# Attention projections taken two groups at a time, 512 columns to a bank, weights in four pieces out of the common slots

## The chip, the core and the metric

The kernel runs on one core of a Trainium2 chip. The metric is the device time of one execution in microseconds (us), median of three runs. The profile is one further execution of the same program, recorded by the hardware profiler. PE is the matrix engine (TensorE), PEld its loading of stationary operands, DVE the vector engine, ACT the scalar engine, POOL GpSimd, SP the queue that issues most DMAs.

## What is computed

One layer of a streaming encoder over 1024 positions of width 1024, in float32. The normalized input is projected to many column groups at once, three token mixers work on them, gates merge their outputs, and a SwiGLU block follows:

```python
h = rms_norm(x, g_mix[l])
z = h @ w_in[l]
aq, ak, av, bq, bk, bv, iq, ik, iw, cx, cy, gt = split_cols(z)
y_a = chunk_relpos_attention(rms_norm(aq), rms_norm(ak), av, rel_bias)      # 4 heads, band of 9 chunks
q_b = apply_rope(rms_norm(bq)); k_b = apply_rope(rms_norm(bk))
score = sum_h w_i[h] * relu(q_i[h] . k_i)                                   # indexer, 4 heads
y_b = attention of q_b over the top 256 keys of score
y_c = rglru_branch(cx, cy, ...)
merged = sum_b sigmoid(gt_b) * (y_b @ w_branch_b)
x = x + merged @ w_out[l]
x = x + (silu(g_) * u_) @ w_ffn_out[l]
```

The change is in the projections of aq, ak, av, bq, bk, bv: six groups of 256 columns.

## The kernel before

Every product is made of three matmuls: both operands are split into a high part (by ACT, L101) and a rest (by DVE, L102), and `mm3` adds high x high, high x rest and rest x high (L117 to L119). A weight piece is loaded by `load_split` (L104): a DMA on the SP queue into a tile "r", then the high part "h" on ACT and the rest "l" on DVE. So a piece of weights named wz appears as wzr (raw), wzh and wzl, each 4 KB to a partition (128x1024).

**Slots.** All such tiles lie in 50 slots. `ring` is a set of 7 for weights alone, `sl` one of 43 for all else: score and relu tiles, softmax tiles P and transposed ones PT, sorted keys, bias and mask tiles, z tiles. A `get` takes the slot that was freed longest ago, a `free` puts it at the end of the list:

```python
i = self.free_list.pop(0)
...
self.free_list.append(i)
```

A tile in a slot waits for the last reader of the tile that had it. `z_group` (L318) takes its two pieces (128x4x256, half of the 1024 input rows each) from `ring`.

**Projection.** `z_batch` (L329) computes four of the eight blocks of 128 positions: two blocks share a PSUM bank of 512 columns as two halves of 256. A block is 24 matmuls of 256 columns (8 input slices by 3). ACT copies a whole bank out (L335). `head_rstd` (L339) then makes the head norms: a square on ACT, a sum on DVE, a power on POOL, a multiplication on DVE. `qk_A` makes queries and keys of two heads of branch A, `v_group` the values, `qk_B` queries and keys of branch B with their rotation. Each is called once for each of the six groups: 6 x 8 x 24 = 1152 matmuls of 256 columns.

**What lies around it.** From about 48 us PE makes the indexer's scores: 24 S tiles of `dots` (L242, L243), two banks in turn; ACT applies relu (L310), DVE weights and adds (L312, L314). The relu tile of one S tile lies in a slot of `sl` until DVE has read it. After that, DVE finds the 256th largest score of each row in 32 rounds of a bitwise search ("K" steps; counts at L643, on ACT at L655), while attention A runs: A0 and A1 are its two pairs of heads, with 8 blocks of 2 heads each. In `attention` (L396) each S tile is read by DVE (L406, adds bias or mask, takes the minimum), ACT takes exp (L409), DVE scales (L412), PE transposes to T banks (L418), ACT copies to PT (L419), PE multiplies with v (L426). Gates ("G" steps, wg weights, 512 columns), branch C, then attention B (B0, B1) follow, then merge and SwiGLU, which is PE work alone with its loads beside it.

**The order.** The string ORDER says which step's program text comes next: K a round of the search, A a block of attention A, G a gate, Z a projection, C, B, T, W, F the rest. The scheduler of the tile framework then orders each engine's instructions within the window that the string gives.

## Time and profile before

| | us |
|---|---|
| median of 3 runs (1515.85 to 1518.37) | 1517.07 |
| the profiled execution itself | 1517.05 |
| its span, from the first to the last instruction | 1515.3 |
| PE busy | 1469.1 |
| DVE busy | 1119.1 |
| ACT busy | 762.9 |

The time of a run is the span and 1.75 us around it. Busy times overlap between engines; those of PE are longer than the spacing of its matmuls, since the next one starts while the last is still draining, so the spacing of starts says what a matmul costs in a stream.

### The profile page before, as it was taken

The page shows a single profiled execution, that of the slowest core. Times are in us where ns is not written, and L with a number is a line of the kernel's source. Part 1 is how long each engine was busy: PE and PEld are TensorE (multiplying, and loading weights), DVE is VectorE, ACT ScalarE, POOL GpSimd, SP SyncE. Part 2 cuts the span into 40 slices and gives each one's busy share as a digit, 9 for nine tenths or more (in the row PEclk, how much of TensorE's full clock was granted, in tenths as well). Part 3 has the DMA queues.
Part 4 walks back from the last instruction along what each step waited for, and adds up shares of the span by engine and source line. Part 5 has one row for each costly group of instructions (what it writes and reads, how often), then busy time and mean ns, then how long its engine had stood idle before and what let it go on. Part 6 is the DMA issues. An engine that isn't in the chain of part 4 may idle for free.

```text
span 1515.3 us, 19935 instructions
## 1 busy us (share of the span) xinstructions
PE 1469.1 (97%) x7556; PEld 1228.5 (81%) x7556; DVE 1119.1 (74%) x1985; ACT 762.9 (50%) x1208; POOL 109.5 (7%) x161
## 2 busy tenths in 40 slices
PE   6999899999999998999999989999999999999999
PEld 5898688989788876788888868888888888888887
DVE  7989999869666779767889776555555556578972
ACT  6557768775778656443214663333333333344340
POOL 1220011210000200110000200000000000000000
PEclk9999999999999999999999999999999999999999
DMA  7011212122111121357552412323232323697532
GB/s 289 29 46 54 87 32 102 39 70 85 56 53 45 42 102 53 125 181 298 216 189 75 153 59 96 111 97 112 98 111 98 111 97 126 230 386 263 190 125 89
DMA packets 52240, 182.59 MB, mean 120 GB/s; under 512 B 6000, under 2 KB 6128, under 8 KB 52144
## 3 DMA queue, kind: packets, MB, share of 16 engines
q1 hardware_dynamic: 38448, 135.17, 25.9%
q0 software_dynamic: 11968, 43.00, 7.2%
q10 hardware_dynamic: 1728, 3.15, 0.5%
q8 instruction: 59, 0.97, 0.3%
q14 instruction: 37, 0.30, 0.1%
HBM read 135.94 MB, written 45.35 MB: 120 GB/s over the span
## 4 chain that ended last, share of the span: by engine, by line
PE 75%; DVE 14%; ACT 5%; issue 3%; DMA 2%; POOL 0%; POOLq 0%; ACTq 0%; SPq 0%; DVEq 0%
PE B L119 15%; PE B L118 15%; PE B L117 15%; PE G L118 7%; PE G L119 7%; PE G L117 6%; DVE key L643 3%; PE T L426 2%; PE T L118 1%; PE T L117 1%; PE T L119 1%; PE T L418 1%; PE S L117 1%; PE S L118 1%; PE S L119 1%
## 5 line engine op out<-in xcount | busy, mean ns | idle before, releaser
L118 PE MATMUL B<-hl,fwh 128*128 128x512 f32 x528 | 205.8, 392 | 1.5 <-DVE hl L1026 1.5
L117 PE MATMUL B<-hh,fwh 128*128 128x512 f32 x528 | 203.4, 393 | 1.6 <-ACT hh L1025 1.3
L119 PE MATMUL B<-hh,fwl 128*128 128x512 f32 x528 | 198.8, 391 | 1.9 <-DVE fwl L102 1.9
L117 PEld LDWEIGHTS B<-hh,fwh 128*128 128x128 f32 x528 | 99.8, 189 | 23.5 <-ACT hh L1025 2.2
L119 PEld LDWEIGHTS B<-hh,fwl 128*128 128x128 f32 x528 | 99.8, 189 | 23.1 <-DVE fwl L102 2.3
L118 PEld LDWEIGHTS B<-hl,fwh 128*128 128x128 f32 x528 | 99.8, 189 | 22.9 <-DVE hl L1026 2.2
L118 PE MATMUL G<-wzl,hTh 128*128 128x256 f32 x384 | 111.3, 290 | 5.3 <-DVE wzl L102 5.3
L117 PE MATMUL G<-wzh,hTh 128*128 128x256 f32 x384 | 110.8, 291 | 1.3 <-ACT wzh L101 0.6
L119 PE MATMUL G<-wzh,hTl 128*128 128x256 f32 x384 | 110.8, 289 | 0.0
L102 DVE TENSOR_TENSOR fwl<-s,fwh 128x1024 fp32r<-128x1024 f32 x44 | 53.7, 1223 | 74.1 <-PE B L118 74.1
L118 PE MATMUL B<-fol,foh 128*128 128x512 f32 x264 | 102.9, 390 | 0.0
L119 PE MATMUL B<-foh,fol 128*128 128x512 f32 x264 | 101.9, 389 | 0.0
L117 PE MATMUL B<-foh,foh 128*128 128x512 f32 x264 | 101.1, 389 | 0.0
L655 ACT ACTIVATE junk_s<-score,ngS 128x1024 int8<-128x1024 f32 (+2 forms) x78 | 77.5, 994 | 17.5 <-DVE ngS L653 13.5
L118 PEld LDWEIGHTS G<-wzl,hTh 128*128 128x128 f32 x384 | 74.6, 194 | 7.1 <-DVE wzl L102 6.1
L119 PE MATMUL G<-hTh,wgl 128*128 128x512 f32 x192 | 75.8, 395 | 2.0 <-DVE wgl L102 2.0
L117 PEld LDWEIGHTS G<-wzh,hTh 128*128 128x128 f32 x384 | 74.6, 195 | 3.2 <-ACT wzh L101 1.1
L117 PE MATMUL G<-hTh,wgh 128*128 128x512 f32 x192 | 75.8, 395 | 0.0
L118 PE MATMUL G<-hTl,wgh 128*128 128x512 f32 x192 | 75.4, 393 | 0.0
L119 PEld LDWEIGHTS G<-wzh,hTl 128*128 128x128 f32 x384 | 74.8, 195 | 0.3 <-issue 0.2
L101 ACT ACTIVATE fw<-fb 128x512 fp32r<-128x512 f32 x22 | 13.9, 632 | 117.0 <-PE B L119 117.0
L101 ACT ACTIVATE foh<-fa 128x1024 fp32r<-128x1024 f32 x33 | 35.0, 1061 | 57.5 <-DMA fa<-pd 37.7
(486 smaller groups left out, 3847.7 us busy)
## 6 DMA issues: line engine op xcount, KB each, us to landing
fw<-in_w_fo SPq DMA_DIRECT2D x33, 512.0 KB, 5.7
fa<-pd SPq DMA_DIRECT2D x33, 512.0 KB, 5.5
gl<-gd SPq DMA_DIRECT2D x24, 512.0 KB, 5.9
fa<-in_w_fi SPq DMA_DIRECT2D x22, 512.0 KB, 3.5
fb<-in_w_fi SPq DMA_DIRECT2D x22, 512.0 KB, 3.6
pd<-act POOLq DMA_DIRECT2D x22, 512.0 KB, 5.3
ga<-in_w_g SPq DMA_DIRECT2D x18, 512.0 KB, 3.6
x<-in_x SPq DMA_DIRECT2D x16, 512.0 KB, 5.9
```

The lines of the kernel that those rows point to most:

```text
L101: S.activation(hi, raw, AF.Copy)
L102: (eng or V).tensor_tensor(lo, raw, hi.bitcast(F32), op=OP.subtract)
L117: PE.matmul(o, lhsT=lh, rhs=rh, start=first, stop=False, **kw)
L118: PE.matmul(o, lhsT=lh, rhs=rl, start=False, stop=False, **kw)
L119: PE.matmul(o, lhsT=ll, rhs=rh, start=False, stop=last, **kw)
L418: PE.transpose(pt[:, b - c0], P[:, 128 * b:128 * b + 128], ident)
L426: PE.matmul(o[64 * e:64 * e + 64, :], lhsT=v[(b0 + b) // 4][:, (b0 + b) % 4, h, :], rhs=PT[e][:, b, :], start=b == 0, stop=b == nb - 1, sk ...
L643: V.tensor_scalar(o[:, 0:(i + 1) * 128], (keys or score)[i], ap[:, j:j + 1], 0.0, op0=op, op1=OP.add, accum_out=self.cnt[:, j:j + 1])
L655: S.activation(junk_s[:, 0:(i + 1) * 128], score[i], AF.Sign, bias=self.ng.bitcast(F32)[:, j:j + 1], accum_out=self.cnt[:, j:j + 1])
```

## The change

`z_group`, `z_batch`, `qk_A`, `v_group`, `qk_B` go. `z_pair` takes two groups together: (q and k of A0, v of A), (q and k of A1, q and k of B0), (v of B, q and k of B1). Its weights come as four pieces (128x2x512, a quarter of the input rows each), the same 12 loads of 512 KB in all, but out of `zw`, which is `sl`: the common slots, with no slots of their own. A block is 24 matmuls of 512 columns into a whole bank, 576 in all. ACT copies each bank out in two copies of 256 columns, 48 in all where there were 24 of 512. The head norms of the first pair come behind the whole pair, and `rope_B` is called where a Z step of B stood. In ORDER some G steps stand later among the K and A steps before the first Z, and one more behind the third Z. The weights' layout on the host follows.

```diff
-ORDER = ("KAAGKKKAKKAKAKKKKKKAGGGAKKKKAYAKGGAGAKKKKKKKAKKKAZ"
-         "AAAKKGKGZKKKKBCBGBCBCBCBBBZBBFBFBGGBBBBTTWFFWWFFWWW")
+ORDER = ("KAAGKKKAKKAKAKKKKKKAGGGAKKKKAYAKAGAKKKKGKKKAKKKGAZ"
+         "AAAKKKGZKKKKBCBGBCBCBCBBBZGBBFBFBGGBBBBTTWFFWWFFWWW")
...
-    def z_group(gi):
-        ws = [load_split(w_zg[gi, kk], (128, 4, 256), "wz") for kk in range(2)]
-        return ws
...
+    def z_pair(gi, names):
+        ws = [load_split(w_zg[gi, q], (128, 2, 512), "wz", zw) for q in range(4)]
+        zs = []
+        for g in range(2):
+            z = [sl.get((128, 4, 4, 64), F32, n) for n in names]
+            for j in range(4):
+                t = 4 * g + j
+                p = gbank()
+                for k in range(KD):
+                    hh, hl = hT[k]
+                    wh, wl = ws[k // 2]
+                    mm3(p, hh[:, 128 * t:128 * t + 128], hl[:, 128 * t:128 * t + 128], wh[:, k % 2], wl[:, k % 2],
+                        k == 0, k == KD - 1)
+                for n in range(2):
+                    S.activation(z[n][:, j].rearrange("p h d -> p (h d)"), p[:, 256 * n:256 * n + 256], AF.Copy)
+            zs.append(z)
+        for wh, wl in ws:
+            zw.free(wh, wl)
+        return [[z[n] for z in zs] for n in range(2)]
...
-    zA = [qk_A(0)]
-    vA = v_group(2)
-    def steps_zA():
-        zA.append(qk_A(1))
+    zw = sl
+    qk0, vA = z_pair(0, ("zA", "v"))
+    zA, zB, vB = [qk0], [], []
+    for z in qk0:
+        head_rstd(z)
+
+    def steps_zA():
+        qk1, b0 = z_pair(1, ("zA", "zB"))
+        for z in qk1:
             head_rstd(z)
...
-        zB.append(qk_B(3, tabs))
+        rope_B(zB[0], tabs)
         yield
-        vB.extend(v_group(5))
+        v, b1 = z_pair(2, ("v", "zB"))
+        vB.extend(v)
         yield
-        zB.append(qk_B(4, tabs))
+        rope_B(b1, tabs)
+        zB.append(b1)
         sl.free(*tabs)
         yield
```

Three places of the engines' orders follow. In these rows a name ends in the number of the buffer or of the instruction that wrote it, and "waits" names what the row waits for.

The first place is PE at the beginning of the indexer's scores. Before, S tiles (S_642, S_648) stand among matmuls of the first projection (G_889), whose weights wzh_11 to wzl_15 came from `ring`:

```order
L119 MATMUL G_889<-wzh_14_834,hTl_14_97 128x256
L117 MATMUL G_889<-wzh_14_834,hTh_15_98 128x256
L242 MATMUL S_642<-kih_39_315,qi_35_311 128x384 [waits Activation_49]
L242 MATMUL S_648<-kih_39_315,qi_36_312 128x384
L118 MATMUL G_889<-wzl_15_835,hTh_15_98 128x256
L119 MATMUL G_889<-wzh_14_834,hTl_16_99 128x256
L117 MATMUL G_889<-wzh_11_828,hTh_1_84 128x256
L118 MATMUL G_889<-wzl_12_829,hTh_1_84 128x256
```

In the changed order the projection's first matmul (G_852, out of wzh_79) comes when 17 of the 24 S tiles (up to S_758) have been issued, and the next ones stand two tiles later, behind wzl_80:

```order
L242 MATMUL S_758<-kih_39_315,qi_35_311 128x512 [waits Activation_49]
L243 MATMUL S_758<-kil_40_316,qi_35_311 128x512
L242 MATMUL S_758<-kih_39_315,qi_35_311 128x384
L243 MATMUL S_758<-kil_40_316,qi_35_311 128x384
L117 MATMUL G_852<-wzh_79_828,hTh_1_84 128x512 [waits Activation_49]
L117 MATMUL G_879<-wzh_79_828,hTh_1_84 128x512
L242 MATMUL S_766<-kih_39_315,qi_36_312 128x512 [waits Activation_49]
```

Here the projection no longer stands between the first 17 S tiles, and two banks of it start together as pieces arrive.

The second place is DVE, where the weight pieces are split (L102). Before, wzl_15 and wzl_18 stand among the rotation of the indexer's queries, ahead of the scores:

```order
L213 TENSOR_TENSOR qi_37_313<-T_461,qi_37_313 64x512 [waits Activation_49]
L102 TENSOR_TENSOR wzl_15_835<-wzr_13_832,wzh_14_834 128x1024 [waits DMAHW6_49,Activation_49]
L213 TENSOR_TENSOR qi_36_312<-T_452,qi_36_312 64x512 [waits Activation_49]
L282 TENSOR_TENSOR zq_45_477<-zq_45_477,t2_48_603 128x1024 [waits DVE_49]
L273 SCALAR_TENSOR_TENSOR zk_46_478<-zk_46_478,rsk_595,sm_68 128x64 [waits Pool_49]
```

Now the splits stand among the scores of the last three blocks of queries, the first with nine score rows to go:

```order
L314 SCALAR_TENSOR_TENSOR score_51_639<-relu_68_746,iw_310,score_51_639 128x768 [waits DVE_49,Activation_49]
L102 TENSOR_TENSOR wzl_80_829<-wzr_78_826,wzh_79_828 128x1024 [waits DMAHW7_49,Activation_49]
L314 SCALAR_TENSOR_TENSOR score_51_639<-relu_69_754,iw_310,score_51_639 128x768 [waits DVE_49,Activation_49]
L312 TENSOR_SCALAR score_52_640<-relu_70_763,iw_310 128x896 [waits Activation_49]
L102 TENSOR_TENSOR wzl_83_835<-wzr_81_832,wzh_82_834 128x1024 [waits DMAHW0_49,Activation_49]
```

The pieces have moved behind the rows that free their slots: wzr_78 is in the slot of relu_63, wzh_79 in that of relu_64, wzl_80 in that of relu_65, each of which DVE reads first.

The third place is PE at the second projection, at the end of A0. Before, its matmuls stand between S tiles (S_2242 is A0's last but one) with the weights of `ring`:

```order
L243 MATMUL S_2242<-kl_94_1413,qs_90_1409 128x256
L119 MATMUL G_2364<-wzh_39_2303,hTl_6_89 128x256
L117 MATMUL G_2364<-wzh_39_2303,hTh_7_90 128x256
L118 MATMUL G_2364<-wzl_40_2304,hTh_7_90 128x256
L119 MATMUL G_2364<-wzh_39_2303,hTl_8_91 128x256
L117 MATMUL G_2314<-wzh_42_2309,hTh_9_92 128x256 [waits Activation_49]
```

In the changed order all of A0's S tiles are ahead of it, and its third piece (wzl_148) stands behind T_2104, the product of A0's last block with v. These are the rows where the fourth piece (wzh_150, wzl_151) comes in:

```order
L118 MATMUL G_2170<-wzl_148_2132,hTh_11_94 128x512
L119 MATMUL G_2170<-wzh_147_2131,hTl_12_95 128x512
L117 MATMUL G_2143<-wzh_150_2137,hTh_13_96 128x512 [waits Activation_49]
L117 MATMUL G_2170<-wzh_150_2137,hTh_13_96 128x512
L118 MATMUL G_2143<-wzl_151_2138,hTh_13_96 128x512 [waits DVE_49]
L119 MATMUL G_2143<-wzh_150_2137,hTl_14_97 128x512
```

So the projection has moved behind A0. The slot of wzr_149 is that of PT_137 and the slot of wzh_150 that of PT_139, both read by T_2104; wzl_151 is in the slot of a bias tile of A0. From wzl_151 on, 154 of this projection's 192 matmuls are still to come, and then the transposes for A1.

## Rows read from the trace of the kernel before

**Rows 1.** The page of the profile: the span, and busy time of each engine.

```profile
span 1515.3 us, 19935 instructions
...
PE 1469.1 (97%) x7556; PEld 1228.5 (81%) x7556; DVE 1119.1 (74%) x1985; ACT 762.9 (50%) x1208; POOL 109.5 (7%) x161
```

**Rows 2.** Stretches: PE, PEld, DVE, ACT, POOL busy (instructions), PE clock, DMA share, GB/s.

```profile
0.00:48.00 48.00, 34.86 (x199) 31.90 (x200) 35.39 (x113) 28.87 (x83) 12.58 (x19) 1.00 0.59 228
48.00:75.00 27.00, 23.74 (x170) 21.47 (x170) 24.66 (x38) 16.80 (x32) 2.82 (x5) 1.00 0.13 40
75.00:119.00 44.00, 44.00 (x342) 42.73 (x341) 39.09 (x105) 23.57 (x32) 9.18 (x9) 1.00 0.15 49
119.00:199.00 80.00, 70.94 (x375) 56.98 (x375) 78.47 (x279) 57.59 (x118) 2.22 (x4) 0.96 0.17 61
188.00:195.60 7.60, 4.46 (x20) 3.79 (x20) 7.60 (x26) 5.09 (x12) 0.00 (x0) 0.72 0.00 1
600.00:1515.00 915.00, 902.74 (x3982) 742.75 (x3981) 626.05 (x798) 350.74 (x444) 45.04 (x85) 1.00 0.42 151
```

**Rows 3.** Timeline of PE, 256 columns: start, duration, engine, line, operation, tiles.

```profile
101.76 0.28 PE L119 MATMUL G<-wzh,hTl 128*128 128x256 f32 x1
...
103.92 0.28 PE L117 MATMUL G<-wzh,hTh 128*128 128x256 f32 x1
```

**Rows 4.** Timeline of PE, matmuls of 512 columns.

```profile
949.81 0.39 PE L118 MATMUL B<-hl,fw 128*128 128x512 f32 x1
...
961.82 0.39 PE L119 MATMUL B<-hh,fwl 128*128 128x512 f32 x1
```

**Rows 5.** Groups of DVE from 75 to 240 us: busy, mean ns, idle before.

```profile
L643 DVE TENSOR_SCALAR_CACHE_REDUCE key<-key,cdV 128x896 bf16<-128x896 bf16 x15 | 17.2, 1143 | 0.1
L643 DVE TENSOR_SCALAR_CACHE_REDUCE key<-key,cdV 128x640 bf16<-128x640 bf16 x15 | 13.1, 876 | 0.2
L643 DVE TENSOR_SCALAR_CACHE_REDUCE key<-key,cdV 128x512 bf16<-128x512 bf16 x15 | 11.2, 745 | 0.1
...
L643 DVE TENSOR_SCALAR_CACHE_REDUCE key<-key,cdV 128x384 bf16<-128x384 bf16 x15 | 9.1, 609 | 0.2
...
L406 DVE CUSTOM_DVE_ANT_0 P<-S,biasA 128x640 f32<-128x640 f32 x8 | 6.6, 820 | 1.2 <-PE T L418 0.7 <-PE T L426 0.6
```

**Rows 6.** Tile wzr: its DVE reader, and issue to landing of its DMA.

```profile
L102 DVE TENSOR_TENSOR wzl<-wzr,wzh x12: 1218/1224/1227, 47.9 to 480.6; 128x1024 fp32r<-128x1024 f32 x12
...
DMA to landing us min/median/max: 3.3/3.5/10.8
```

**Rows 7.** Groups of ACT from 0 to 600 us: two copies out of a bank.

```profile
L335 ACT ACTIVATE zA<-G 128x512 f32<-128x512 f32 x8 | 4.6, 598 | 1.1 <-PE G L119 1.1
...
L260 ACT ACTIVATE zq<-G 128x256 f32<-128x256 f32 x8 | 3.1, 382 | 10.9 <-PE G L119 10.9
```

**Rows 8.** Timeline of DVE, score rows of one block of 128 queries.

```profile
71.76 2.87 DVE L314 SCALAR_TENSOR_TENSOR score<-relu,iw,score 128x640 f32<-128x640 f32 x3
```

**Rows 9.** Timeline of DVE, second S tile of A0's seventh block.

```profile
193.33 0.82 DVE L406 CUSTOM_DVE_ANT_0 P<-S,biasA 128x640 f32<-128x640 f32 x1
```

**Rows 10.** Timeline of PE, first S tiles of A1 and of B0.

```profile
239.59 0.28 PE L242 MATMUL S<-kh,qs 128*128 128x256 f32 x1
...
369.85 0.28 PE L242 MATMUL S<-kh,qs 128*128 128x256 f32 x1
```

**Rows 11.** Timeline of PE, first and last S tile of B1.

```profile
535.68 0.28 PE L242 MATMUL S<-kh,qs 128*128 128x256 f32 x1
...
577.62 0.47 PE L242 MATMUL S<-kh,qs 128*128 128x512 f32 x1
```

**Rows 12.** Timeline of PE, a wait for a weight piece, and matmuls behind it.

```profile
193.40 0.39 PE L118 MATMUL G<-wzl,hTh 128*128 128x256 f32 x1 [3.13 <-DVE wzl L102]
...
194.13 0.41 PE L119 MATMUL G<-wzh,hTl 128*128 128x256 f32 x1
194.34 0.41 PE L117 MATMUL G<-wzh,hTh 128*128 128x256 f32 x1
```

More of the change, by code (lines that the diff above doesn't have):

```diff
@@ L317, in hybrid_kernel @@
     sl.free(*qi, kih, kil, ctab)
-    def z_group(gi):
-        ws = [load_split(w_zg[gi, kk], (128, 4, 256), "wz") for kk in range(2)]
-        return ws
-    def z_mm(ws, p, t):
-        for k in range(KD):
-            hh, hl = hT[k]
-            wh, wl = ws[k // 4]
-            mm3(p, hh[:, 128 * t:128 * t + 128], hl[:, 128 * t:128 * t + 128], wh[:, k % 4], wl[:, k % 4],
-                k == 0, k == KD - 1)
-    def z_batch(ws, g, name):
-        z = sl.get((128, 4, 4, 64), F32, name)
-        for a in range(2):
-            p = gbank((128, 2, 256))
-            for j in range(2):
-                z_mm(ws, p[:, j], 4 * g + 2 * a + j)
-            S.activation(z[:, 2 * a:2 * a + 2].rearrange("p t h d -> p (t h d)"), p.rearrange("p t c -> p (t c)"),
-                         AF.Copy)
-        return z
+    def z_pair(gi, names):
[17 more added lines that the diff above has]
+        return [[z[n] for z in zs] for n in range(2)]
     def head_rstd(z):
@@ L365, in to_stack @@
         return q, kh, kl
-    def done(ws):
-        for wh, wl in ws:
-            ring.free(wh, wl)
     ga8 = const.tile([128, 1], F32, name="ga8")
     V.tensor_scalar(ga8, smc("ga", 0), 0.125, None, op0=OP.mult)
-    def qk_A(gi):
-        ws = z_group(gi)
-        r = []
-        for g in range(2):
-            z = z_batch(ws, g, "zA")
-            head_rstd(z)
-            r.append(z)
-        done(ws)
-        return r
-    def v_group(gi):
-        ws = z_group(gi)
-        r = [z_batch(ws, g, "v") for g in range(2)]
-        done(ws)
-        return r
-    zA = [qk_A(0)]
-    vA = v_group(2)
-    def steps_zA():
-        zA.append(qk_A(1))
+    zw = sl
[6 more added lines that the diff above has]
+        for z in qk1:
+            head_rstd(z)
+        zA.append(qk1)
+        zB.append(b0)
         yield
@@ L564, in bm, with rope_B @@
         return ap[:, None, :].to_broadcast([128, n, ap.shape[-1]])
-    def qk_B(gi, tabs):
-        ws = z_group(gi)
-        r = []
-        for g in range(2):
-            z = z_batch(ws, g, "zB")
+    def rope_B(zs, tabs):
+        for g, z in enumerate(zs):
             head_rstd(z)
@@ L579, in qk_B @@
             V.tensor_add(z, z, t2)
-            r.append(z)
             sl.free(t2)
-        done(ws)
-        return r
     def steps_zB():
@@ L1475, in _layout @@
     pair = lambda q, k, p: np.concatenate([blk(q + 128 * p, 128), blk(k + 128 * p, 128)], 2)
-    zg = [pair(COL_AQ, COL_AK, 0), pair(COL_AQ, COL_AK, 1), blk(COL_AV, 256),
-          pair(COL_BQ, COL_BK, 0), pair(COL_BQ, COL_BK, 1), blk(COL_BV, 256)]
-    zg = np.stack([a.reshape(128, 2, 4, 256).transpose(1, 0, 2, 3) for a in zg])
+    zg = [(pair(COL_AQ, COL_AK, 0), blk(COL_AV, 256)), (pair(COL_AQ, COL_AK, 1), pair(COL_BQ, COL_BK, 0)),
+          (blk(COL_BV, 256), pair(COL_BQ, COL_BK, 1))]
+    zg = np.stack([np.concatenate(a, 2).reshape(128, 4, 2, 512).transpose(1, 0, 2, 3) for a in zg])
     wc = np.stack([blk(c + 128 * n, 128) for n in range(4) for c in (COL_CX, COL_CY)])
```

1 line of the change is left out of this document (removed).

## Prediction

> **What bounds the kernel now.** The page comes first: PE is busy for 1469.1 of 1515.3 us, DVE for 1119.1 [rows 1]. The sum is made against the profiled run's own 1517.05 us, which is the median to 0.02. Then the stretches, to see where PE is not full [rows 2]. From 600 us to the end PE has 902.7 of 915 us: one stream, in which nothing can be made up. From 75 to 119 it is full, too. From 119 to 199, in A0, it has 70.9 of 80 while DVE has 78.5: there DVE sets the pace, since PE may issue an S tile only when DVE has read the one two tiles earlier. Up to 75 us DVE has 35.4 + 24.7 = 60.1 us of work, so it has idled 14.9; by 199 us it has 177.6, so it has idled 21.4, only 6.5 more.
>
> So I keep two accounts at each checkpoint: when PE reaches it, and how much PE work stands behind it. PE work is counted in matmuls at the spacing of their starts in a stream: 19 matmuls of 256 columns from 101.76 to 103.92 are 18 steps of 120 ns [rows 3], 54 of 512 columns from 949.81 to 961.82 are 53 steps of 227 ns [rows 4]. The other sizes are equally many in both kernels and, unless I say so, equally many ahead of a checkpoint.
>
> **The stream itself.** 1152 matmuls of 256 columns become 576 of 512: 576 x (2 x 120 - 227) ns = 7.5 us less PE work. This is the gain if all waits stay as they are. The Trainium skill, page "TensorE: Matmul & The Clock Gate", section "Back-to-back issue gap", gives 262 and 518 cycles at 2.4 GHz for an isolated gap at these widths: by it the gain would be 576 x (2 x 109.2 - 215.8) = 1.5 us, an estimate, and the sum 6 us higher. The rows above are slower than that at both widths, and the sum goes by the rows.
>
> **The copies out of the banks.** ACT had 24 of 598 ns and gets 48 at about 382, the price of 256 columns [rows 7]: 18.3 instead of 14.4 us. PE fills the other bank for 24 x 227 ns = 5.4 us meanwhile, so both copies (0.76) are hidden. I take nothing; uncovered it would be the 4 us. The head norms of A0 behind the whole pair cost what they did, and lie beside the search. DMAs are 12 of 512 KB before and after, 3.5 us each from issue to landing, and 12 splits on DVE of 1.22 [rows 6].
>
> **First place: the scores.** The first 17 S tiles now have no projection among them, and what is between them is DVE's pace: a block of 640 columns takes 2.87 us for three of its four rows [rows 8]. The pieces of the first pair sit in slots of relu tiles, so they come only as DVE gets through the scores, one after the other until about its last block. PE, which had 23.7 us of work between 48 and 75 us [rows 2], then has S tiles and a few transposes, by my count about half of that. The first pair therefore runs mostly after 75 us, and A0 starts later. DVE isn't idle: its order puts 9 rounds of the search ahead of the first tile of A0, where it had 2.
>
> **Through A0.** There the price shows on DVE; its work ahead of a row is summed over its order, each instruction at the mean duration of its form. Ahead of its row for the second S tile of A0's seventh block stand 19 rounds, where 14 stood: one more on sorted keys of 1.14 + 0.88 + 0.75 + 0.61 = 3.4 us [rows 5] and four without the 640 columns, 2.5 each, with small operations of some 2 us in all; two splits of wz fewer and two of wg more cancel. That is 15 us more work. Before, DVE reached that row at 193.33 [rows 9]. With the same idle time it reaches it at 208.4; if it never idles behind 75 us, the 6.5 fall away: 201.9.
>
> **Second place: the second pair.** Its last piece waits for slots that A0's last block frees. In DVE's order the last split (wzl_151) has 25.3 us of work between the row above and itself: six rounds of 2.5, three splits of 1.22, three tiles of 0.82 with their scalings, small ones. So it starts at 227.2 to 233.7 and ends 1.2 later. Whether its DMA (3.5 us behind the product with v) and the copy on ACT come later than that, no row of before shows; they can add up to 4, and nothing if the search covers them, which I take, since six rounds stand there. Behind this split PE still has, before the first S tile of A1, 187 matmuls of 512 columns (154 of the projection, 33 of gates), 42.4 us, and 0.9 of others. A1 starts at 271.7 to 278.2 us; I take 275. Before it started at 239.59 [rows 10].
>
> What is behind that row? Ahead of it stand 40 matmuls of 256 and 653 of 512 columns, before 616 and 293, and 4 transposes fewer: 360 x 0.227 - 576 x 0.12 - 0.4 = 12.2 us more done. With the 7.5 of the stream, 19.7 less remains. So at A1 the change is 275 - 239.6 - 19.7 = +15.7 us, from +12.4 to +22.9.
>
> **From A1 to B0.** The same PE work stands between the two first S tiles, 121.4 us; before, it took 369.85 - 239.59 = 130.3 [rows 10], 8.9 of waits. Two things pull against each other: all 32 rounds are over, which freed DVE; but the third pair's pieces wait for P and PT of A1, a bias tile and yA behind its store, and ahead of them stands A1's second half with no filler, some 18 us of PE against 24 of DVE. I take 10 us of waits, bounds 6 and 15: +1 (-3 to +6).
>
> **B1.** Ahead of its first S tile, PE has done more again, and between first and last S tile it has 14.6 us of work where it had 37.8 in 41.9 [rows 11], 4.1 of waits. The attention's own chain on DVE is some 21 us and can't be shortened: 22 to 26 us pass, 8 to 11 of them waits. I take +4 (+2 to +8).
>
> **Sum.** 15.7 + 1 + 4 = +21: 1517.05 + 21 = 1538 us. The ends of the terms give +11 and +37; both ends together are unlikely, and I take +13 to +35, 1530 to 1552, as this case's own range. A difference under 0.2%, 3 us, could not be told from none.
>
> **Rivals.** *The cover holds (faster).* Gates and attention fill PE where the projection left, and DVE had 6.5 us to spare from 75 to 199. If the waits at every place are no more than before, only the stream's 7.5 us are left: 1509.5. It decides at A1: at 239.6 + 19.7 = 259.3 us the two kernels are level. DVE alone has 242 us of work ahead of it there, and with the 14.9 it had idled by 75 us that is 257. So it would need DVE without a gap and a second pair whose pieces come 15 us earlier in DVE's order than they stand. I give it 0.11, with what lies between it and no change.
>
> *The slots come free in time, DVE alone decides.* A1 at 257 to 263: -2 to +4, with +1 and +4 behind, less the 4 if gates fill B1: 1516 to 1526. For it: the wait for a piece was short before, 3.13 us at its worst in A0 [rows 12]. Against it: the pieces' place in DVE's order is fixed, behind the rounds. 0.11, half of it within 3 us.
>
> *The clock falls.* From 188 to 195.6 us PE was busy 4.46 of 7.6 us and its granted clock was 0.72 [rows 2]; behind the 3.13 us wait its matmuls of 256 columns start 0.21 us apart, not 0.12, the lower of the two levels (1.2 and 2.4 GHz) [rows 12]. The change makes many such gaps. The Trainium skill, same page, section "HAM oscillation — how this bites in real kernels", describes matmuls in short bursts between waits for data that start at the low clock each time; the rows agree as far as they go. Where DVE is late anyway that costs nothing; if a quarter to a half of one pair's 43.6 us runs at half speed on the path, it adds 11 to 22: 1549 to 1560. 0.12.
>
> **Chances.** The forecast has 0.66. Faster 0.11, within 3 us 0.06, slower 0.83. From 1514 to 1554 leaves out most of the first rival and the upper half of the last, and the forecast's own tails, 2 in 10 together.
>
> **What would show it.** In the profile of the changed kernel: z matmuls 0.227 us apart; PE with under 15 us of work from 48 to 75 us; A1's first S tile at 272 to 278 us, behind a wait of PE for wzl of several us; DVE over 95% busy from 75 to 230. If A1 starts before 260 us, the forecast is wrong at the second place; if it starts at 275 and the time is still not over 1525, waits behind A1 have been given back, and the rounds that are done early paid for it; if B0 is later than 121 + 15 us behind A1, the third pair was dearer than I took.

## The result, and the profile of the changed kernel

The changed kernel takes 1609.69 us, the median of 4 runs (1607.69 to 1612.01), beside 1517.72 of the kernel before (4 runs, 1515.85 to 1519.61): a ratio of 1.0606, 95% interval 1.0593 to 1.0618. It is slower, as forecast, but by 92 us, not by 21.

The page of the changed kernel, against [rows 1]:

```profile
span 1610.2 us, 18849 instructions
...
PE 1500.7 (93%) x6980; PEld 1218.3 (76%) x6980; DVE 1120.0 (70%) x1985; ACT 768.0 (48%) x1232; POOL 113.0 (7%) x161
...
PEclk9899989978989899999999999999999999999999
```

The span is 94.9 us longer. DVE and ACT have almost as much to do as before: DVE +0.9, ACT +5.1, of which the copies out of the banks make 4.0 (18.1 us against 14.1). PE shows 31.6 us more busy time although its work fell; the mean granted clock, 0.964 where it was 0.994, is one reason: part of its matmuls ran at the lower level. The row of PEclk falls below 9 only in the first 14 of 40 slices, up to about 560 us.

Stretches of the changed kernel, columns as in [rows 2]:

```profile
48.00:75.00 27.00, 18.67 (x77) 13.93 (x77) 24.76 (x40) 16.61 (x30) 3.71 (x6) 0.75 0.15 52
...
319.00:362.00 43.00, 28.70 (x174) 22.55 (x172) 24.93 (x47) 17.76 (x36) 14.13 (x12) 0.79 0.23 64
...
444.00:647.00 203.00, 174.39 (x859) 138.79 (x858) 122.53 (x165) 125.79 (x175) 15.94 (x14) 0.92 0.16 55
...
671.00:1610.00 939.00, 923.58 (x4176) 758.86 (x4174) 650.56 (x832) 367.96 (x479) 45.52 (x86) 1.00 0.42 148
```

The stretches of A1's second half and of B0 in the kernel before:

```profile
268.00:318.00 50.00, 50.00 (x373) 44.80 (x373) 41.91 (x113) 38.15 (x82) 12.33 (x12) 1.00 0.14 44
...
370.00:536.00 166.00, 163.16 (x942) 135.50 (x941) 114.42 (x154) 120.97 (x170) 11.43 (x11) 1.00 0.16 56
```

PE is emptier in three stretches: it is busy for 18.67 of 27 us during the scores, where it had 23.74 [rows 2], for 28.70 of 43 at 319 us, where it had 50 of 50, and for 174.39 of 203 in B0, where it had 163.16 of 166. From 671 on it has 923.58 of 939. In the first of these DVE is nearly full, 24.76 of 27, as it was. In the other two it is not: 24.93 of 43, 122.53 of 203. So neither engine is the bound there; each waits for the other.

The timeline of PE in the changed kernel: first S tile of A1, z matmuls, first S tile of B0, first and last of B1:

```profile
285.31 0.28 PE L242 MATMUL S<-kh,qs 128*128 128x256 f32 x1
...
391.21 0.39 PE L117 MATMUL G<-wzh,hTh 128*128 128x512 f32 x1
...
396.65 0.39 PE L117 MATMUL G<-wzh,hTh 128*128 128x512 f32 x1
...
443.68 0.28 PE L242 MATMUL S<-kh,qs 128*128 128x256 f32 x1
...
646.84 0.36 PE L242 MATMUL S<-kh,qs 128*128 128x256 f32 x1
...
670.72 0.48 PE L242 MATMUL S<-kh,qs 128*128 128x512 f32 x1
```

The matmuls from 391.21 to 396.65 are 24 steps of 227 ns. The S tiles are the checkpoints of the prediction [rows 10, 11]. Between them I count PE's work as the prediction did (each matmul at the spacing of its size in a stream); time less work is waiting, matmuls at half speed included:

| stretch | before: time, work, waits | after: time, work, waits | waits more |
|---|---|---|---|
| start to A1 | 239.6, 197.6, 42.0 | 285.3, 209.8, 75.5 | +33.5 |
| A1 to B0 | 130.3, 121.4, 8.8 | 158.4, 121.4, 37.0 | +28.2 |
| B0 to B1 | 165.8, 156.2, 9.6 | 203.2, 158.3, 44.8 | +35.2 |
| B1, first to last S tile | 41.9, 37.8, 4.2 | 23.9, 14.6, 9.3 | +5.1 |
| the rest | 937.7, 913.3, 24.4 | 939.5, 914.7, 24.8 | +0.4 |

The waits rise by 102.4 us and the work falls by 7.5: +94.9, the difference of the spans. So there are three large places, not one: ahead of A1, in A1's second half (of the 28.2, 19.8 lie between A1's ninth and last S tile, where the waits are 22.2 us now and were 2.4; the other 8.4 are not followed up here), and in B0 with branch C.

**The first place** is the one that was forecast. Timeline of the changed kernel: DVE's read of the second S tile of A0's seventh block, then the way of the second pair's last piece, then matmuls of this projection:

```profile
207.02 0.82 DVE L394 CUSTOM_DVE_ANT_0 P<-S,biasA 128x640 f32<-128x640 f32 x1
...
231.75 1.31 PE L414 MATMUL T<-PT,v 128*64 128x128 f32 x20
...
233.13 0.33 SPq L107 DMA_DIRECT2D wzr<-in_w_zg  x1
...
237.06 1.06 ACT L101 ACTIVATE wzh<-wzr 128x1024 fp32r<-128x1024 f32 x1 [1.84 <-DMA wzr<-in_w_zg]
...
238.15 1.23 DVE L102 TENSOR_TENSOR wzl<-wzr,wzh 128x1024 fp32r<-128x1024 f32 x1 [1.70 <-ACT wzh L101]
...
238.17 1.22 PE L117 MATMUL G<-wzh,hTh 128*128 128x512 f32 x2 [2.58 <-ACT wzh L101]
...
243.43 0.63 PE L119 MATMUL G<-wzh,hTl 128*128 128x512 f32 x1
...
243.86 0.63 PE L117 MATMUL G<-wzh,hTh 128*128 128x512 f32 x1
...
245.16 0.40 PE L118 MATMUL G<-wzl,hTh 128*128 128x512 f32 x1
...
245.39 0.39 PE L119 MATMUL G<-wzh,hTl 128*128 128x512 f32 x1
```

DVE is at that row at 207.02. The product with v (231.75) frees the slot, SP issues the load at 233.13, ACT's copy begins at 237.06 as the data lands, DVE's split at 238.15, and PE has waited 2.58 us. Between the row at 207.02 and this split DVE has 25.8 us of work and is idle for 5.3, of which 4.3 stand in front of the splits of the second pair's four pieces. The matmuls behind the wait start 0.43 us apart until 244.3, and 0.23 us from 244.9 on: the granted clock was at the lower level (0.50, 1.2 GHz) from 237.9 to 244.6, after PE had worked in short bursts between waits, and at the higher one (1.00, 2.4 GHz) from 244.7 on.

**The second place** is A1's second half. The waits of DVE from 319 to 362 us (in total, times, longest), then the waits of PE there:

```profile
DVE s L343 <- ACT sq L341: 5.2, 2, 4.6
DVE P L394 <- PE T L406: 5.2, 2, 3.1
DVE P L394 <- PE T L414: 3.3, 1, 3.3
DVE zB L347 <- POOL r L127: 2.7, 1, 2.7
```

```profile
PE T L414 <- ACT PT L407: 4.2, 3, 3.4
PE S L242 <- DVE nm L394: 4.0, 2, 2.5
PE T L406 <- DVE rc L399: 3.1, 1, 3.1
```

DVE waits 8.5 us here for A1's own transposes and products on PE (T), and 7.9 for the head norm of zB, B0's queries and keys, whose rotation `rope_B` stands in the order at the first Z of B. The timeline shows why the norm is slow to come:

```profile
332.98 0.55 POOL L569 DMA_DIRECT2D cs<-in_cs  x1 [15.57 <-ACT yA L416]
...
338.73 1.22 DVE L343 TENSOR_REDUCE s<-sq 128x16 f32<-128x1024 f32 x1 [0.59 <-ACT sq L341]
...
346.62 5.81 POOL L127 TENSOR_TENSOR r<-rs_v,mhalf 128x16 f32<-128x16 f32 x2
...
349.57 1.24 DVE L347 TENSOR_TENSOR zB<-zB,r 128x1024 f32<-128x1024 f32 x1 [2.67 <-POOL r L127]
```

POOL issues the load of the rotation's table at 332.98, behind 15.57 us of waiting for ACT's yA; it builds tables up to 346, and only then come its two powers for the norm, 5.81 us. DVE's multiplication with them starts at 349.57, 10 us after its sum over the squares. A1's minima (nm, L394) and scalings stand behind these waits in DVE's order, and PE behind them: the reciprocal for one P is done at 346.9, but its scaling (L400) begins at 350.73, behind that multiplication.

The same norms and rotations stood among A1's last blocks before. The timeline of DVE in the kernel before shows the second of them, with a wait for the same power:

```profile
303.51 1.21 DVE L343 TENSOR_REDUCE s<-sq 128x16 f32<-128x1024 f32 x1
...
308.03 1.23 DVE L347 TENSOR_TENSOR zB<-zB,r 128x1024 f32<-128x1024 f32 x1 [2.27 <-POOL r L127]
```

There it cost PE almost nothing, since PE had the projection of B0's queries and keys and gates to do beside it: 47.5 us of counted work between A1's ninth and last S tile, where it has 21.2 now. So two things meet here: a chain of a later stage in DVE's order, and the projection that covered it gone, which the second pair has made already.

**The third place** is B0. The waits of PE from 444 to 647 us, and the timeline of the longest:

```profile
PE G L117 <- ACT u L505: 11.2, 2, 5.7
PE S L520 <- ACT lwh L101: 4.2, 1, 4.2
```

```profile
525.64 1.22 DVE L540 TENSOR_TENSOR u<-u,ge 128x1024 f32<-128x1024 f32 x1
...
527.39 0.53 POOL L541 DMA_DIRECT2D yd<-u  x1 [42.79 <-DVE u L540]
...
530.39 1.45 ACT L505 ACTIVATE u<-G,sm 128x512 f32<-128x512 f32 x2 [4.57 <-DMA yd<-u]
...
531.22 0.80 PE L117 MATMUL G<-hTh,wcyh 128*128 128x512 f32 x1 [5.72 <-ACT u L505]
```

A block of branch C makes a tile u (ACT copies it out of a bank, L505; DVE multiplies it at the end, L540), stores it with a DMA that POOL issues, and frees its slot. Here the next block's u got that same slot: ACT's copy waits 4.57 us until the store has left, the bank stays full, and PE stands for 5.72 us in front of the next product. In the kernel before, PE's waits from 370 to 536 us have none for u, and its granted clock there is 1.00. I followed the slots through both programs: when the first block of C takes its tiles, 11 slots are free before, 9 in the changed kernel, where two zB tiles of B1 already lie in the others; a block takes 8. Before, four blocks' u get four different slots; after, the second, third and fourth get the same one.

### The profile page after: what moved, and what is told of

The parts are those of the page before. It is cut to its first block, busy times and chain, and to the rows that moved or that the text cites. A ratio compares the mean times of both kernels' runs of the same rounds, so it can differ in the third digit from the quotient of the medians.

```text
span 1610.2 us, 18849 instructions
## 1 busy us (share of the span) xinstructions
PE 1500.7 (93%) x6980; PEld 1218.3 (76%) x6980; DVE 1120.0 (70%) x1985; ACT 768.0 (48%) x1232; POOL 113.0 (7%) x161
## 4 chain that ended last, share of the span: by engine, by line
PE 56%; DVE 5%; issue 3%; ACT 2%; POOL 0%; DMA 0%; DVEq 0%; ACTq 0%; POOLq 0%
PE B L119 14%; PE B L118 14%; PE B L117 14%; PE G L119 2%; PE G L117 2%; PE G L118 2%; PE T L118 1%; PE T L119 1%; PE T L117 1%; PE S L117 1%; PE S L119 1%; PE S L118 1%; DVE tq L772 1%; DVE hl L1008 0%; PE T L414 0%
## 5 line engine op out<-in xcount | busy, mean ns | idle before, releaser
L102 DVE TENSOR_TENSOR fwl<-s,fwh 128x1024 fp32r<-128x1024 f32 x44 | 53.7, 1224 | 72.9 <-PE B L118 70.3
L117 PE MATMUL G<-wzh,hTh 128*128 128x512 f32 x192 | 77.0, 412 | 8.2 <-ACT wzh L101 8.2
L118 PE MATMUL G<-wzl,hTh 128*128 128x512 f32 x192 | 78.5, 409 | 1.4 <-DVE wzl L102 1.4
L119 PE MATMUL G<-wzh,hTl 128*128 128x512 f32 x192 | 77.4, 403 | 0.0
L1204 DVE TENSOR_TENSOR act<-act,B 128x512 f32<-128x512 f32 x22 | 15.1, 687 | 65.6 <-PE B L119 65.6
L414 PE MATMUL T<-PT,v 128*64 128x128 f32 x528 | 50.5, 312 | 10.4 <-ACT PT L407 10.4
L406 PE MATMUL T<-ident,P 128*128 128x128 f32 x264 | 47.8, 302 | 12.9 <-ACT PT L407 6.0
```

Of the source, the lines that this page charges most:

```text
L102: (eng or V).tensor_tensor(lo, raw, hi.bitcast(F32), op=OP.subtract)
L117: PE.matmul(o, lhsT=lh, rhs=rh, start=first, stop=False, **kw)
L118: PE.matmul(o, lhsT=lh, rhs=rl, start=False, stop=False, **kw)
L119: PE.matmul(o, lhsT=ll, rhs=rh, start=False, stop=last, **kw)
L406: PE.transpose(pt[:, b - c0], P[:, 128 * b:128 * b + 128], ident)
L414: PE.matmul(o[64 * e:64 * e + 64, :], lhsT=v[(b0 + b) // 4][:, (b0 + b) % 4, h, :], rhs=PT[e][:, b, :], start=b == 0, stop=b == nb - 1, sk ...
```

## Theories

*Slots.* The loss is one of slots: pieces of weights in the common list come late and push back every tile behind them, and tiles that are made early and held leave too few free. *Cover.* The loss is one of order: the projection in wide blocks, and the steps as ORDER puts them, leave PE nothing to do while attention goes through DVE; slots would only show as the last of several waits. *Clock.* The low clock makes most of it. In the experiments, us beside a ratio are its distance from 1, or from the ratio of the other kernel named, times 1518.

## Experiments on order, slots and width

**The order alone** (e1): the kernel before with the new string.

```diff
-ORDER = ("KAAGKKKAKKAKAKKKKKKAGGGAKKKKAYAKGGAGAKKKKKKKAKKKAZ"
-         "AAAKKGKGZKKKKBCBGBCBCBCBBBZBBFBFBGGBBBBTTWFFWWFFWWW")
+ORDER = ("KAAGKKKAKKAKAKKKKKKAGGGAKKKKAYAKAGAKKKKGKKKAKKKGAZ"
+         "AAAKKKGZKKKKBCBGBCBCBCBBBZGBBFBFBGGBBBBTTWFFWWFFWWW")
```

> The kernel before with only the string ORDER of the change; groups, widths and slots as before. Theory 1 (slots: the weight pieces and the z tiles that are made early crowd the 43 common slots, and later tiles wait for the slots of tiles that are in use) and theory 2 (lumps: three projections of 44 us each instead of six of 23 leave stretches of attention with no other work for the matrix engine) both expect that a string with a few gate steps moved costs little here: within 10 us of 1517. Theory 3 (the string itself starves the stretches) expects most of the 92 us: 1560 or more.

1.0081 (1.0066 to 1.0096): +12 us, a little over the 10 that slots and cover allowed. The new string costs something with the old blocks too, but an eighth of the loss. Most of it, 11 us, lies in B0.

**The slots alone** (e2): the kernel before, 256 columns as they were, pieces from the common slots.

```diff
-        ws = [load_split(w_zg[gi, kk], (128, 4, 256), "wz") for kk in range(2)]
+        ws = [load_split(w_zg[gi, kk], (128, 4, 256), "wz", sl) for kk in range(2)]
...
-            ring.free(wh, wl)
+            sl.free(wh, wl)
```

> The kernel before with only the place of the projections' weights changed: the two pieces of a group come from the common slots instead of the ring. Theory 1 expects a good part of the loss: 20 to 60 us more than 1517, with waits of the matrix engine for wzh and wzl, above all at the scores and behind A0, and perhaps again a u tile of branch C in the slot of one that is still being stored. Theory 2 expects little, since the lumps are as before: under 10 us more.

1.0289 (1.0272 to 1.0306): +44 us, without a wide block or a step moved. Up to A1 the waits are 62.6 us, 20.6 more than before; 13 more come between A1 and B0 and 11 in B0. PE's waits from 48 to 254 us in this kernel:

```profile
PE T L295 <- DVE qi L213: 6.1, 1, 6.1
PE T L426 <- ACT PT L419: 5.5, 4, 3.0
```

The longest is not for a weight but for the indexer's queries (qi). These are not late: DVE makes that row at 52.73 us, at 52.62 in the kernel before. What is gone is the first projection, which PE did meanwhile; its pieces now come behind the scores. The changed kernel has the same wait, 6.1 us.

**The changed kernel with slots of its own for the weights** (e3): the two that make 9 of the 7 of `ring`, three pieces at a time.

```diff
-    zw = sl
+    ring.free_list += [sl.free_list.pop(0) for _ in range(2)]
+    zw = ring
```

> The changed kernel with the four pieces from the ring, which gets two of the common slots for it (9 and 41) once the scores are issued; widths, string and steps as in the change. Theory 1 expects the waits for weight pieces to go, and with them those of the 102 us that hang on pieces: about 35 to 60 us less than 1610, so 1550 to 1575; what is left is crowding of the 41 common slots. Theory 2 expects that the second half of A1 and the whole of B0 are as empty as before: no more than 25 us less, so 1585 to 1610.

1.0276 (1.0252 to 1.0299), 50 us less than the change, the largest effect of all runs. A1 comes at 260 us, not 285; of the 33.5 us of waits ahead of it 8.6 stay. And 42 us of the whole loss stay: A1's second half still has 24 us of waits, B0 27. So slots for pieces are most of the first place and no more than a part of the others.

**The width alone** (e7): the changed kernel with two rows of 24 matmuls of 256 columns, one for each half of the bank.

```diff
-                for k in range(KD):
...
+                for c in (slice(0, 256), slice(256, 512)):
+                    for k in range(KD):
...
+                        mm3(p[:, c], hh[:, 128 * t:128 * t + 128], hl[:, 128 * t:128 * t + 128], wh[:, k % 2, c],
+                            wl[:, k % 2, c], k == 0, k == KD - 1)
```

> The changed kernel with its pairs, pieces and slots, but each block as two groups of 24 matmuls of 256 columns into the halves of the bank, one half after the other. It prices the width alone: by the spacings of 120 and 227 ns the stream is 7.5 us longer, 1617; by the Trainium skill's figures in 'TensorE: Matmul & The Clock Gate', section 'Back-to-back issue gap', it would be 1.5 us longer, 1611. As waits decide much of this kernel, anything from 1605 to 1625 says no more than that the width is worth little.

1.0717 (1.0701 to 1.0733): 17 us slower than the change, just over the range that I gave. Timeline of PE in this kernel:

```profile
399.75 0.28 PE L117 MATMUL G<-wzh,hTh 128*128 128x256 f32 x1
...
401.19 0.28 PE L117 MATMUL G<-wzh,hTh 128*128 128x256 f32 x1
```

12 steps of 120 ns, as in [rows 3]. So the wide matmul is worth its 7.5 us of PE's work; the other 9 are waits, in which the same projections on the path are longer, and no run separates them.

**Only the first pair wide** (e8): the kernel before, its own order, `z_pair` for the first pair out of 9 slots, two of which go back to the common list after it. Each piece of the single groups comes in two DMAs, as their columns lie in the layout of the pairs.

```diff
-    zA = [qk_A(0)]
-    vA = v_group(2)
+    ring.free_list += [sl.free_list.pop(0) for _ in range(2)]
+    zw = ring
+    qk0, vA = z_pair(0, ("zA", "v"))
+    sl.free_list += [ring.free_list.pop(0) for _ in range(2)]
```

> The kernel before, its string too, but for the first pair (q and k of A0 with v of A), which is taken at 512 columns with four pieces from a ring of 9; the two slots go back to the common ones after it, and all later groups are single ones of 256 columns from the ring. The stream is 2.5 us shorter than before. Theories 1 and 2 both expect the loss of the change to be gone: 1510 to 1525. If the width or the four pieces cost by themselves, at the scores and at A0's beginning, it is 1530 or more.

1.0025 (1.0015 to 1.0036): +4 us. A wide block at the beginning costs almost nothing when it has its slots and gives them back. What costs is what the other pairs and the common slots do.

## Experiments on B0

**Two tiles u held through branch C** (e4), used in turn, in the changed kernel:

```diff
+        up = [sl.get((128, T), F32, "u") for _ in range(2)]
...
-            u = sl.get((128, T), F32, "u")
+            u = up[c % 2]
...
-            sl.free(u, tr, ti, a0, ge)
+            sl.free(tr, ti, a0, ge)
...
-                sl.free(*lw)
+                sl.free(*lw, *up)
```

> The changed kernel with two tiles u held through branch C and used in turn, so that a new u waits for the store of the one two blocks earlier, not for that of the one just finished. In the changed kernel's trace the third and fourth block each show the matrix engine waiting 5.7 us for the copy that writes u, and that copy waiting for the store of u. Theory 1 in this form expects 10 to 15 us less: 1595 to 1600. If these waits only stand for the lack of other work (theory 2), the time moves to the next wait and is within 4 us of 1610.

1.0514 (1.0489 to 1.0538): 14 us less than the change. PE no longer waits for u in B0, and the waits of B0 go from 45 to 36: the store is in the path, but it is not all of B0. The profiled executions differ by more, 18.0 us, and 8.1 of these are there by 391 us, where both kernels have had the same instructions in the same order on every engine; A1 begins at 278.48 here, at 285.31 in the change. So an edit's effect is read in its own place, here 9 us in B0, and a place read from one profile can move by several us from one execution to the next. Why it does is not shown.

**Two common slots fewer in the kernel before** (e5), given to `ring` with nothing else changed:

```diff
+    ring.free_list += [sl.free_list.pop(0) for _ in range(2)]
     zA = [qk_A(0)]
```

> The kernel before with two of the 43 common slots given to the ring once the scores are issued (9 and 41); nothing else. It prices the loan that run e3_new_ring9 made. If crowding of the common slots alone makes the rest of that run's loss (1559.75 against 1518.7), this takes 25 us or more: 1543 to 1560. If the rest comes from the lumps (theory 2), the loan is cheap: under 10 us, 1519 to 1529.

1.0228 (1.021 to 1.0245): +35 us. The waits of B0 are 41 us where they were 9.6. No wide block, no new order, and B0 is nearly as bad as in the change.

**The same with two tiles u held** (e9), as above:

```diff
+    ring.free_list += [sl.free_list.pop(0) for _ in range(2)]
...
+        up = [sl.get((128, T), F32, "u") for _ in range(2)]
```

> e5_old_ring9 (the old kernel with two common slots fewer, 1553.71) with two tiles u held through branch C and used in turn. That run showed the matrix engine waiting 12.2 us for copies into u, all of its loss being within B0. If the loss comes from one bad meeting in the list of free slots (a new u gets the slot of the u that is being stored), most of it goes: 1525 to 1538, though the two held tiles leave the list one shorter still. If it comes from crowding as such, it stays at 1550 or more.

1.0129 (1.0114 to 1.0144), 15 us less, just above the range that I gave for one bad meeting; PE's wait for u falls from 12.2 to 1.0 us. But 20 of the 35 us stay without that wait. How much of them is the price of the two tiles held, which leave the list shorter still, no run separates.

**Two tiles u held in the changed kernel with 9 slots** (e10):

```diff
+    ring.free_list += [sl.free_list.pop(0) for _ in range(2)]
+    zw = ring
...
+        up = [sl.get((128, T), F32, "u") for _ in range(2)]
```

> e3_new_ring9 (1559.75) with the two u tiles in turn. Its trace has 5.2 us of waits for copies into u; with the clock that falls behind them, 8 to 14 us less are expected where the meeting of slots is the cause: 1546 to 1552. Within 4 us of 1560 otherwise.

1.0431 (1.0416 to 1.0447), 24 us slower than with 9 slots alone, against what I expected. PE's waits from 402 to 616 us in this kernel, and timeline of ACT:

```profile
PE G L117 <- ACT u L507: 19.0, 3, 9.8
```

```profile
491.41 0.60 ACT L506 ACTIVATE xc<-G 128x512 f32<-128x512 f32 x1 [4.01 <-DVE u L537]
...
531.71 0.60 ACT L506 ACTIVATE xc<-G 128x512 f32<-128x512 f32 x1 [3.62 <-DVE u L537]
```

Two tiles that are held are two slots less for the rest: now xc, the other tile of a block of C, gets a slot that DVE reads until the scan of the block before (L537) is through. ACT makes xc ahead of u, so the copy into u is late as well, and PE waits 19.0 us for it where it waited 5.2 without the held tiles. The wait moved from one tile to the next, and grew.

**One slot or two put aside** (e13 and e14), in the kernel before, until the merge:

```diff
+    held = [sl.free_list.pop(0) for _ in range(1)]
     zA = [qk_A(0)]
...
+    sl.free_list += held
     rl = ring.free_list
```

> The kernel before with one common slot put aside from the end of the scores until its merge stage; ring, widths, string as before. In its order the third and fourth u of branch C still get slots whose last reader is the vector engine, not a store. If the count of free slots acts through meetings with late readers, this costs little: 1518 to 1530. If each slot has its price (crowding), about half of e5_old_ring9's 35 us: 1532 to 1540.

> The same with two common slots put aside, the ring still 7. Now the third u gets the slot of the u that is being stored. If the common slots made e5_old_ring9's loss, this comes out as that run did: 1545 to 1560, with waits for the copy into u and all of the loss within B0. If the longer ring made it, 1518 to 1530.

With one fewer 1.0044 (1.0027 to 1.0061), +7 us; with two 1.0252 (1.0235 to 1.0269), +38, as much as with two given to `ring`. The first slot is nearly free, the second is not. PE's longest waits from 370 to 580 us, one slot fewer and then two fewer:

```profile
PE S L533 <- DVE us L213: 2.7, 3, 1.5
```

```profile
PE G L117 <- ACT u L518: 10.6, 2, 5.7
```

And timeline of ACT, two fewer:

```profile
465.50 1.45 ACT L518 ACTIVATE u<-G,sm 128x512 f32<-128x512 f32 x2 [4.59 <-DMA yd<-u]
...
503.78 1.45 ACT L518 ACTIVATE u<-G,sm 128x512 f32<-128x512 f32 x2 [3.74 <-DMA yd<-u]
```

With 42 common slots PE doesn't wait for u. With 41, the picture of the changed kernel is there: ACT waits for the store of u, PE for ACT, 5.7 us at the longest. B0 begins 3.2 us later than before and B1 43.4 later, so the loss lies between these two.

**The third pair as two single groups** (e6), in the changed kernel with 9 slots, the second group only where B1's projection stood before, its pieces in two DMAs each as in e8:

```diff
-        v, b1 = z_pair(2, ("v", "zB"))
-        vB.extend(v)
+        vB.extend(z_one(2, 0, "v"))
         yield
+        b1 = z_one(2, 1, "zB")
         rope_B(b1, tabs)
```

> As e3_new_ring9, but the third pair is taken apart again: v of B at its step and q and k of B1 at the last Z step, 256 columns each, weights from the ring, so that there is projection work within B0 again. Theory 2 expects the waits within B0 to go, 15 to 25 us less than 1559.75 though its stream is 2.5 us longer: 1535 to 1547. If B0's waits come from slots alone, it stays within 6 us of 1560.

1.0397 (1.0381 to 1.0412), 18 us slower than with the pair, which neither theory expected. Windows of this kernel, in B1:

```profile
591.00:640.00 49.00, 48.59 (x254) 38.21 (x253) 32.91 (x79) 27.57 (x61) 2.17 (x4) 1.00 0.26 87
```

B1 is full now, and 47.2 us pass from first to last S tile where it was 30.3 with the pair: some 17 us of PE's work has moved behind its first S tile. But B1 begins at 590.75, 1.0 us later than with the pair. So the waits ahead of it have grown by about as much; those for u from 5.2 to 10.9 us. As far as this run goes, B0's loss is not the price of taking the third pair at once.

## Experiments on A1's second half

**The rotation of B0's queries and keys one Z step later** (e11), in the changed kernel:

```diff
-        rope_B(zB[0], tabs)
         yield
         v, b1 = z_pair(2, ("v", "zB"))
         vB.extend(v)
+        rope_B(zB[0], tabs)
```

> The changed kernel with the rotation and norms of B0's queries and keys moved from the first Z step to the second, behind the third pair. In the changed kernel's trace the second half of A1 has 22 us of waits of the matrix engine, the vector engine's reading of A1's S tiles standing behind these norms (2.7 us for the power on GpSimd, 4.6 for the square) and rotations. If that place is the cause, 10 to 20 us go: 1590 to 1600, unless the same work is now awaited at B0's first tile. If the cause is that A1's second half has no other work (theory 2), the time stays within 5 us of 1610.

1.0512 (1.0492 to 1.0532), 14 us less. PE's waits from 316 to 345 us in this kernel:

```profile
PE T L414 <- ACT PT L407: 2.9, 2, 2.6
PE T L406 <- ACT PT L407: 0.5, 1, 0.5
```

The waits between A1's ninth and last S tile are 8.1 us, not 22.2, and those behind nm and rc are gone. PE has no more work in this stretch than in the change, so it is not better cover that helps: the norm and rotation on DVE were what A1 stood behind. The other runs agree. With the old single groups, of which 18 to 24 us of projection lie there (e1, e2, e5, e8, e9, e13, e14), these waits are 1 to 11 us though the norms stand there too; with the second pair and the rotation at its place (e3, e4, e6, e7, e10) 22 to 25, with 0 to 12 us of projection; with the second pair and the late rotation (e11, e12, e15) 7 to 8. Some 5 us come back as waits in B0.

**All three** (e12): 9 slots, two u held, late rotation.

```diff
+    ring.free_list += [sl.free_list.pop(0) for _ in range(2)]
+    zw = ring
...
+        up = [sl.get((128, T), F32, "u") for _ in range(2)]
...
-        rope_B(zB[0], tabs)
...
+        rope_B(zB[0], tabs)
```

> The changed kernel with all three: four pieces from a ring of 9, two u tiles in turn, rotation of B0 behind the third pair. If the three causes are separate, their gains add: 1610 less 50 less 10 less what run e11_new_late_rotation shows, 1530 to 1550; it would have to lose 33 us more to beat the kernel before, which none of the theories expects.

1.0347 (1.0329 to 1.0365): 11 us slower than 9 slots alone, and outside the range for gains that add. And **9 slots with the late rotation** (e15), without the held u:

```diff
+    ring.free_list += [sl.free_list.pop(0) for _ in range(2)]
+    zw = ring
...
-        rope_B(zB[0], tabs)
...
+        rope_B(zB[0], tabs)
```

> The changed kernel with the ring of 9 (e3_new_ring9, 1559.75) and the late rotation of e11_new_late_rotation, but u as in the change. If the two gains add (50 and 12 us), 1543 to 1551. If the late rotation meets B0 there, as the waits of e12_new_all_three within B0 suggest, no gain: 1556 to 1566.

1.0283 (1.0268 to 1.0299), no gain over 1.0276. PE's waits for u from 365 to 590 us in this kernel:

```profile
PE G L117 <- ACT u L506: 10.0, 3, 4.9
```

In A1's second half 17 us of waits went, and from B0's third block to B1 they rose by 10; for u PE now waits 10.0 us, 5.2 without the late rotation. Single gains of 50, 14 and 14 don't add. The list of slots is one queue: what is freed later or earlier at one place decides which tile meets which at the next. No version made here is faster than the kernel before.

## Why the prediction was right in direction and wrong in size

In the prediction's own terms, the change came out as +26.0 us at A1 (forecast +15.7), +28.2 from A1 to B0 (+1), +35.2 from B0 to B1 (no term), +5.1 in B1 (+4) and +0.4 behind it. So the step that failed is the waits behind A1: the term for A1 to B0 was far too small, and B0 itself was put at nothing.

**The stream itself**, 7.5 us: right. A matmul takes 227 ns, and the counted work is 1426.3 us before and 1418.8 after. By the figures of the Trainium skill that the prediction weighed (page "TensorE: Matmul & The Clock Gate", section "Back-to-back issue gap") it would have been 1.5, an estimate; the rows decide against it.

**The copies**: right; they take 18.1 us of ACT, forecast 18.3, and PE doesn't wait for them.

**First place and through A0**: right. DVE reached the row named at 207.02, forecast 201.9 to 208.4. PE's counted work from 48 to 75 us is some 11 us, forecast under 15. DVE was busy for 146.7 of 155 us from 75 to 230, 94.7%, where the sign was over 95%.

**Second place, the second pair**: the mechanism right, its size too small. The mis-sized term is that DMA and ACT "can add up to 4, and nothing if the search covers them, which I take". DVE's work from the row named to the last split was as summed, 25.8 us for 25.3, but it stood idle for 5.3 us on the way, mostly for this pair's pieces: the load is issued only behind the product with v, and the split starts at 238.15, 4.5 us behind the latest time forecast. Behind it PE did not run at full speed, which the sum did not have at all: some 2.4 us until 244.3 (12 matmuls by 0.2). A1 came at 285.31, 10.3 later than I took. Not all of that is the term: with the same order up to there, e11 came to A1 at 282.98 and e4 at 278.48, with 5.7 and 3.7 us of idle time on that way. e3, where the pieces don't lie in the common slots, gives 25 us of A1 back.

**From A1 to B0**: wrong. "I take 10 us of waits, bounds 6 and 15": it was 37.0. I priced pieces of the third pair and a stretch without filler, 24 us of DVE against 18 of PE, as if DVE would only have A1 to serve. The missing filler was right. But the norm and rotation of B0's tiles, through ACT, POOL and a table's load, stand in DVE's order among A1's last blocks, and they have no term. They stood there before, too, where the projection hid them; it was to be asked what the filler had hidden. e11 shows the price by moving them: 14 us. The sign for a third pair dearer than taken (B0 more than 121 + 15 us behind A1) came, at 158.4, but 19.8 us of the 28.2 lie ahead of that pair's first matmul.

**B0 to B1**: the largest miss, since the sum has no term for it, and nothing is implied but zero. It was +35.2. I had asked where the weights' pieces get their slots from, and not who lives on those that they leave. e5 and e14 show it in the kernel before, with nothing but two slots taken: 35 and 38 us, of which e9 gives 15 back by holding u. In the changed kernel u shows the same wait, and e4 gives 9 of the 35 back in B0. Of the other waits there, 4.2 us for lwh are for a weight of branch C whose raw tile took the slot of a count tile of the masks (cj), which had followed a wzl in it: its load is issued at 452.11, behind ACT's last read of cj, where it was issued at 366.3 before. The rest is spread over many small ones. What part of the 35 is slots and what the thinner cover, is not told apart beyond this; the new order alone has 11 us of loss in the same place.

**B1**: right, 9.3 us of waits, forecast 8 to 11.

**The rival of the clock** named a true thing at about its price, 11 to 22 us, but as a way of its own. It is a part of each place: counting matmuls that start at the spacing of the lower level while the granted clock was 0.50, I estimate 21 us lost by it after and 6 before, so 15 of the 102. The other 87 are waits; the clock alone is not the cause. The first two rivals are refuted by the checkpoint: by them A1 was to start before 263 us.

Of the theories, slots hold for the first place (e2, e3), and in the kernel before two of them are enough to set B0 off (e5, e14); cover holds for A1's second half in a particular form: work of a later stage stands in DVE's order, and the projection that hid it is gone (e11). Neither alone explains the sum, and the parts don't add.

Left open: the waits of B0 besides u and the weight of branch C, some 20 of its 35 us; the 8.4 us between A1's last S tile and B0; the 9 us beyond the stream with 256 columns; and how much would be left at a full clock.

## What to carry to other kernels

When a change takes buffers from a shared first-in-first-out list, or holds tiles longer, go through every later stage that draws on the list and ask which tile now meets which reader or store; the price isn't proportional: here one of 43 slots less cost 7 us, two cost 35 to 38, of which 15 came back when the store no longer stood between two blocks. When steps are laid out anew, ask of each engine what stands in its order between two instructions of the stage that is bound, above all chains over several engines for a later stage, and what work hides them today: when that work moves away, their delay comes to light. And a term that isn't in the sum is a claim of zero: write it down for each stage, with the row that says so.

## What the runs showed of the hardware that I had not expected

After a wait of 2.58 us the matmuls of 512 columns ran at the lower level, 0.43 us apart, up to 244.3, and after 5.72 us of waiting (531.22) again, up to 534.8, before they came back to 0.23. In the second case the granted clock was 0.50 already ahead of that wait, from 521.2 to 525.4, behind a wait of 1.68 us that ended at 520.59. The Trainium skill, page "TensorE: Matmul & The Clock Gate", section "HAM oscillation — how this bites in real kernels", tells of bursts between waits for data that begin at the low clock each time; these rows agree. The slow matmuls behind each of the two waits cost about 2 us (some 12 and 8 by 0.2); in e4, behind a wait of 2.77 us at the same place, they cost about 1 us.

A tile of 512 KB that is stored holds its slot 3.5 us longer than the instruction that fills it: the multiplication ends at 526.9, POOL issues the store at 527.4, and the next writer begins at 530.39. A power over 128x16 values on POOL takes 2.9 us (two in 5.81; the spans of POOL are rough, but DVE's multiplication with the first begins 2.95 us behind its start), more than twice the 1.22 us that DVE takes for the sum over 128x1024 ahead of it.
